# Stacked queries and keys in DRAM, fetched by one transfer per operand on SyncE's queue

## The chip, the cores and the metric

The kernel runs on one core of a Trainium2 chip. The metric is the device time of one execution in microseconds (us). The kernel before takes 1608.62 us, the median of 3 runs from 1608.35 to 1609.47 us.

## What is computed

Two encoder layers over 512 positions of 1024 channels in float32. Each layer normalizes its input, projects it once, and gives the parts to three branches: differential attention, a convolution module and Fourier mixing. The branches are projected, merged with sigmoid gates, projected again and added to the input; a SwiGLU feed-forward part follows. The change concerns the attention, which is, cut to what matters:

```python
q = u[..., o:o + WIDTH_A].reshape(b, s, N_HEADS_A, 2, D_COMP_A)   # 8 heads, 2 components of 32
k = ...                                                           # the same shape
q = apply_partial_rope(rmsnorm(q, qnorm_g[l]), cos, sin)
k = apply_partial_rope(rmsnorm(k, knorm_g[l]), cos, sin)
sc = jnp.einsum('bqhcd,bkhcd->bhcqk', qi, k) * scale
p = jax.nn.softmax(sc, axis=-1)
w = p[:, :, 0] - lam * p[:, :, 1]
att = jnp.einsum('bhqk,bkhe->bqhe', w, vf)
```

A head thus has two components of 32 channels, each with scores of its own.

## The kernel before

**Precision.** Matmuls run on float32 data that are rounded to a shorter format (`F32R`). Every operand is split into a high part, rounded by ScalarE (ACT), and a low part, the remainder, taken by VectorE (DVE); a product is the sum of high times high, high times low and low times high. For most products these are three matmuls that accumulate in one PSUM bank. For the scores it is one matmul: a component has only 32 channels, so three blocks of 32 are stacked on the 96 partitions of the operand. The queries are stacked as high, low, high and the keys as high, high, low, and one matmul of contraction 96 gives the three products' sum.

**How the stack is made.** `qk_post` normalizes and rotates queries (which = 0) and keys (which = 1), and four steps `turn(gp)`, one for each pair of heads, transpose 128 channels to a tile of 128 channels by 512 positions, split it into two `at` tiles (L163 on ACT, L164 on DVE), and store each to a DRAM tile `dqk` of its own (L849, 256 KB). `stack(h)` then fills, for each of a head's two components, a tile `qst` and a tile `kst`: each by three loads of 32 rows of 512 (L866, 64 KB), one for each block. In all there are 32 stores and 192 loads over the two layers, 12 loads for a head. All of them are issued by SyncE (SP), one instruction after the other.

**What shares SP's queue.** `chunk` loads the weights in chunks of 512 KB (`wr`, L204) from the same queue. A chunk is split too: ACT rounds it (L209). For even chunks DVE takes the remainder (L211). For odd chunks of the part with attention, ACT writes the negative of the rounded chunk (L331) and GpSimd (POOL) issues a transfer that adds the weights to it in place (`wl`, L332). POOL's transfers have a DMA queue of their own (q0 in the profile), those of SP another (q1).

**Buffers.** There are 3 buffers each of `qst` and `kst`, 5 of `at`, 3 of `wr`. A head needs two of `qst` and two of `kst`, so a load waits until TensorE (PE) has used up an older tile: the tiles of a head's first component can be fetched while the head before is still at work, those of its second component only when the head before lets a tile go, shortly before they are used. The `at` buffers go round: after the last stores they serve the exponentials of the scores (L951 on ACT), which must wait until the stores from the buffer have landed.

**What sets the order.** Each engine takes its instructions in the order in which the program's scheduler wrote them, and waits in that order. Attention is woven into the matmuls of the Fourier branch and of the gates: heads start at fixed places between those, `load(h)` is placed ahead of the first scores of head h, and on PE the score matmul `s<-kst,qst` (L127, called from `scores`) stands between matmuls `main<-X,wh` that have nothing to do with it. PE can't go past it. SP's instructions also wait for semaphores that eight lanes share (`DMAHW0` to `DMAHW7` below), each of which an earlier transfer of the same lane must have released.

Of the kernel before, what the change touches and what calls it, by code (L numbers as in the profile page):

```python
# [9 lines left out]
F32 = mybir.dt.float32  # L10
# [6 lines left out]
P = 128  # L17
L = 2
D = 1024
T = 512  # L20
# [15 lines left out]
QS = ("sync",) * 4  # L36
# [58 lines left out]
class Hybrid:  # L95
# [693 lines left out]
    def qk_post(self, l, which, banks):  # L789
        nc = self.nc  # L790
        qs = []
        names = ("rq", "rqs") if which == 0 else ("rk", "rks")
        tabs = []
        for i in range(2):
            tab = self.small(NT * 8, f"tab{i}")
            nc.vector.tensor_tensor(
                out=tab.rearrange("p (t d) -> p t d", d=8), in0=self.rope[:, i],
                in1=self.par(l, names[i]).unsqueeze(1).to_broadcast([P, NT, 8]), op=ALU.mult,
            )
            tabs.append(tab)  # L800
        for tt in range(NT):
            q = self.slot("A")
            nc.scalar.copy(q, banks[tt])
            sq = self.slot("M")
            nc.scalar.activation(sq, q, AF.Square)
            q3 = q.rearrange("p (m d) -> p m d", d=DC)
            sums = self.small(16, f"qs{tt}", 1)
            f = self.small(16, f"qf{tt}", 1)
            fa = self.small(16, f"qa{tt}", 1)
            nc.vector.tensor_reduce(  # L810
                out=sums, in_=sq.rearrange("p (m d) -> p m d", d=DC), axis=AX.X, op=ALU.add
            )
            nc.scalar.activation(f, sums, AF.Abs_reciprocal_sqrt, bias=self.eps, scale=1.0 / DC)
            nc.vector.tensor_scalar(
                out=sums, in0=sums, scalar1=1.0 / DC, scalar2=EPS, op0=ALU.mult, op1=ALU.add
            )
            nc.vector.scalar_tensor_tensor(out=fa, in0=f, scalar=-0.5, in1=f, op0=ALU.mult, op1=ALU.mult)
            nc.vector.tensor_tensor(out=fa, in0=fa, in1=sums, op=ALU.mult)
            nc.vector.scalar_tensor_tensor(out=f, in0=fa, scalar=1.5, in1=f, op0=ALU.add, op1=ALU.mult)
            nc.vector.tensor_tensor(  # L820
                out=q3, in0=q3, in1=f.unsqueeze(2).to_broadcast([P, 16, DC]), op=ALU.mult
            )
            ta3 = self.small(P, "ropea", RB).rearrange("p (m d) -> p m d", d=8)
            tb3 = self.small(P, "ropeb", RB).rearrange("p (m d) -> p m d", d=8)
            c8 = tabs[0][:, tt * 8 : (tt + 1) * 8].unsqueeze(1).to_broadcast([P, 16, 8])
            nc.vector.tensor_tensor(out=ta3, in0=q3[:, :, 0:8], in1=c8, op=ALU.mult)
            for o, i in ((0, 4), (4, 0)):
                s4 = tabs[1][:, tt * 8 + o : tt * 8 + o + 4].unsqueeze(1).to_broadcast([P, 16, 4])
                nc.vector.tensor_tensor(out=tb3[:, :, o : o + 4], in0=q3[:, :, i : i + 4], in1=s4, op=ALU.mult)
            nc.vector.tensor_tensor(out=q3[:, :, 0:8], in0=ta3, in1=tb3, op=ALU.add)  # L830
            qs.append(q)
        gc = self.small(1, f"gc{which}")
        self.after(nc.vector.tensor_scalar_mul(
            gc, self.par(l, "gkc" if which else "gqc"), 1.0 if which else DC ** -0.5
        ))
        out = []

        def turn(gp):
            ps = self.bank("att")
            for tt in range(NT):  # L840
                self.pin(
                    nc.tensor.transpose(  # L842
                        ps[:, tt * P : (tt + 1) * P], qs[tt][:, gp * P : (gp + 1) * P], self.ident
                    )
                )
            pair = []
            for i, src in enumerate(self.split_to(ps, "at", scale=gc)):
                d = self.dram.tile([P, T], F32, tag=f"qk{which}{gp}{i}", name=self.nm("dqk"))
                getattr(nc, QS[1]).dma_start(d, src.bitcast(F32))  # L849
                pair.append(d)  # L850
            out.append(pair)

        for gp in range(4):
            self.later(self.t + QKT + gp * 2000, "qk", lambda gp=gp: turn(gp))
        return out

    def stack(self, h):
        hp, h2 = divmod(h, 2)
        out = []
        for c in range(2):  # L860
            row = []
            for which, order in ((0, (0, 1, 0)), (1, (0, 0, 1))):
                dst = self.slot("kst" if which else "qst", F32R)
                lo = h2 * 64 + c * 32
                for r, hl in enumerate(order):
                    getattr(self.nc, QS[0]).dma_start(  # L866
                        dst[r * 32 : (r + 1) * 32, :].bitcast(F32), self.scr[which][hp][hl][lo : lo + 32, :]
                    )
                row.append(dst)
            out.append(row)  # L870
        return out
# [458 lines left out]
```

## Time and profile before

| | us |
|---|---|
| median of 3 runs | 1608.62 |
| the profiled execution | 1605.44 |
| its span, first to last instruction | 1603.7 |
| PE busy in the span | 1585.8 (99%) |
| DVE busy | 1307.9 (82%) |
| ACT busy | 869.9 (54%) |

The profiled execution's time lies 1.74 us above its span and 3.2 us below the median. In the profile an engine's name is followed by the line of the kernel, the operation, and the tiles (written<-read). PE is the matmul part of TensorE, PEld its weight load; SPq and POOLq are the parts of SP and POOL that issue transfers. A transfer has a start (its issue) and a landing. The granted clock of TensorE was 0.999 in the mean.

### The profile page before, as it was taken

Reading aid. Unit: us, or ns where it says so; the run is one execution under the profiler, and the core shown is the slowest. Engines: PE = TensorE matmul, PEld = TensorE weight load, DVE = VectorE, ACT = ScalarE, POOL = GpSimd, SP = SyncE. Lnnn points to the kernel's source line nnn. Section 1 sums busy time; section 2 is a strip of 40 time slices with the busy share of each in tenths; the row PEclk is TensorE's granted clock in tenths of the full one; section 3 lists DMA queues with packets and bytes.
Section 4 is the critical chain, followed back from the end, with each engine's and each line's share of the span. In section 5 each row is a group of like instructions: output and inputs, shape, how many; then the busy total and the mean of one; then the engine's idle time right before and its main releaser. Section 6 shows DMA issues by size and latency. Waiting matters only on the chain.

```text
span 1603.7 us, 24440 instructions
## 1 busy us (share of the span) xinstructions
PE 1585.8 (99%) x9104; PEld 1387.5 (87%) x9104; DVE 1307.9 (82%) x2388; ACT 869.9 (54%) x1419; POOL 183.5 (11%) x162
## 2 busy tenths in 40 slices
PE   9999999999999999999999999999999999999999
PEld 7888888787889898999888888887878898989998
DVE  6999999785897786858779999986758978778684
ACT  6546566873575453635443565568635754536351
POOL 1000010113330000000200000020233300000000
PEclk9999999999999999999999999999999999999999
DMA  6557365454554554547432664555455635546361
GB/s 223 170 164 202 79 164 150 117 132 112 165 149 115 146 134 140 139 109 191 123 118 81 192 186 113 135 146 125 107 120 155 167 94 156 133 133 158 90 159 66
DMA packets 80471, 222.85 MB, mean 139 GB/s; under 512 B 11216, under 2 KB 12368, under 8 KB 80352
## 3 DMA queue, kind: packets, MB, share of 16 engines
q1 hardware_dynamic: 67392, 175.59, 34.9%
q0 software_dynamic: 12528, 45.17, 16.2%
q8 instruction: 72, 1.18, 0.3%
q10 hardware_dynamic: 432, 0.53, 0.1%
q14 instruction: 47, 0.39, 0.1%
HBM read 207.35 MB, written 13.89 MB: 138 GB/s over the span
## 4 chain that ended last, share of the span: by engine, by line
PE 95%; DVE 2%; DMA 1%; ACT 1%; issue 0%; SPq 0%; ACTq 0%
PE main L127 57%; PE s L343 9%; PE main L343 9%; PE att L343 8%; PE s L127 4%; PE att L127 3%; PE oth L127 3%; PE att L137 2%; DMA wraw<-in_w 0%; PE att L842 0%; DVE A L161 0%; DMA kst<-dqk 0%; SPq L866 0%; DMA wr<-in_w 0%; PE oth L137 0%
## 5 line engine op out<-in xcount | busy, mean ns | idle before, releaser
L209 ACT CAST wh<-wr 128x1024 fp32r<-128x1024 f32 x178 | 186.1, 1049 | 244.4 <-PE main L127 127.3
L127 PE MATMUL main<-X,wh 128*128 128x512 f32 x864 | 278.4, 395 | 0.0
L211 DVE TENSOR_TENSOR wl<-wr,wh 128x1024 fp32r<-128x1024 f32 x138 | 176.6, 1280 | 36.7 <-ACT wh L209 36.1
L127 PEld LDWEIGHTS main<-X,wh 128*128 128x128 f32 x864 | 160.8, 188 | 32.3 <-issue 0.3
L1127 DVE SCALAR_TENSOR_TENSOR cv<-cv,hcw,cv 128x497 f32<-128x497 f32 (+14 forms) x240 | 180.2, 751 | 0.9
L127 PE MATMUL main<-X,wl 128*128 128x512 f32 x432 | 169.7, 393 | 0.0
L127 PE MATMUL main<-act,wh 128*128 128x512 f32 (+1 forms) x520 | 161.8, 391 | 0.0
L951 ACT ACTIVATE at<-s,mx 128x512 f32<-128x512 f32 x128 | 87.9, 688 | 58.1 <-DVE mx L949 49.1
L127 PEld LDWEIGHTS main<-act,wh 128*128 128x128 f32 x520 | 96.2, 188 | 21.7 <-DVE M L652 0.6
L127 PE MATMUL main<-A,wh 128*128 128x512 f32 x320 | 107.7, 393 | 0.0
L127 PE MATMUL main<-att,wh 128*128 128x512 f32 x320 | 100.0, 393 | 3.0 <-ACT att L160 3.0
L310 POOL DMA_DIRECT2D wlo<-in_w x44 | 37.7, 857 | 561.8 <-DVE V L653 166.2
L949 DVE TENSOR_REDUCE mx<-s 128x1 f32<-128x512 f32 x128 | 86.5, 682 | 18.5 <-PE s L127 17.9
L127 PE MATMUL main<-act,wl 128*128 128x512 f32 (+1 forms) x260 | 101.4, 391 | 0.0
L127 PE MATMUL main<-wh,X 128*128 128x512 f32 x288 | 96.7, 392 | 0.0
L127 PEld LDWEIGHTS main<-X,wl 128*128 128x128 f32 x432 | 81.4, 188 | 16.5
L332 POOL DMA_DIRECT2D wl<-in_w x40 | 34.5, 862 | 518.8 <-ACT wl L331 357.1
L127 PE MATMUL main<-cv,wh 128*128 128x512 f32 x240 | 76.8, 392 | 0.0
L127 PEld LDWEIGHTS main<-att,wh 128*128 128x128 f32 x320 | 59.7, 188 | 17.4 <-ACT att L160 3.5
L127 PE MATMUL main<-A,wl 128*128 128x512 f32 x192 | 74.4, 390 | 0.0
L127 PEld LDWEIGHTS main<-A,wh 128*128 128x128 f32 x320 | 59.7, 188 | 11.9
L127 PEld LDWEIGHTS main<-wh,X 128*128 128x128 f32 x288 | 53.9, 188 | 11.1
(371 smaller groups left out, 4190.4 us busy)
## 6 DMA issues: line engine op xcount, KB each, us to landing
wr<-in_w SPq DMA_DIRECT2D x222, 512.0 KB, 3.8
wlo<-in_w POOLq DMA_DIRECT2D x44, 512.0 KB, 5.6
wl<-in_w POOLq DMA_DIRECT2D x40, 512.0 KB, 7.7
cv<-in_w SPq DMA_DIRECT2D x80, 256.0 KB, 4.9
dqk<-at SPq DMA_DIRECT2D x32, 256.0 KB, 4.7
qst<-dqk SPq DMA_DIRECT2D x96, 64.0 KB, 2.3
kst<-dqk SPq DMA_DIRECT2D x96, 64.0 KB, 2.0
V<-in_xT SPq DMA_DIRECT2D x8, 256.0 KB, 6.9
```

Source lines behind the costliest of these rows:

```text
L127: return self.pin(self.nc.tensor.matmul(out, lhsT=lhsT, rhs=rhs, start=start, stop=stop))
L137: self.pin(self.nc.tensor.transpose(ps[:, s], src[:, s], self.ident))
L209: nc.scalar.copy(hi, raw)
L211: nc.vector.tensor_tensor(out=lo, in0=raw, in1=hi.bitcast(F32), op=ALU.subtract)
L310: nc.gpsimd.dma_start(l2, src2, accum_op=ALU.add)
L332: self.nc.gpsimd.dma_start(lo, src, accum_op=ALU.add)
L343: self.nc.tensor.matmul(ps, lhsT=a[:, s], rhs=b, start=start and k == ks[0] and i == 0, stop=last and i == 2, skip_group_check=True,)
L949: nc.vector.tensor_reduce(out=mx, in_=ps, axis=AX.X, op=ALU.max, negate=True)
L951: nc.scalar.activation(e, ps, AF.Exp, bias=mx, accum_out=z1 if c else z0)
L1127: ins = nc.vector.scalar_tensor_tensor(out=acc[:, a:b], in0=g[:, a + d : b + d], scalar=w[:, t : t + 1], in1=acc[:, a:b], op0=ALU.mult, op ...
```

## The change

`turn(gp)` stores into one DRAM tile of three blocks of 128 rows, in the order in which the stack wants them: high, low, high for queries, high, high, low for keys. The high part is therefore stored twice: three stores of 256 KB for each pair of heads and operand, 48 in all in place of 32. `stack(h)` then fetches each `qst` and each `kst` tile by one transfer of 192 KB: 64 loads in place of 192. Its source is a pattern of 3 blocks by 32 rows by 512 numbers, where the blocks lie 256 KB apart, and its destination 96 partitions by 512. Queue and engine stay the same, and so does everything else.

```diff
-            pair = []
-            for i, src in enumerate(self.split_to(ps, "at", scale=gc)):
-                d = self.dram.tile([P, T], F32, tag=f"qk{which}{gp}{i}", name=self.nm("dqk"))
-                getattr(nc, QS[1]).dma_start(d, src.bitcast(F32))
-                pair.append(d)
-            out.append(pair)
+            pair = self.split_to(ps, "at", scale=gc)
+            d = self.dram.tile([3, P, T], F32, tag=f"qk{which}{gp}", name=self.nm("dqk"))
+            for r, i in enumerate((0, 0, 1) if which else (0, 1, 0)):
+                getattr(nc, QS[1]).dma_start(d[r], pair[i].bitcast(F32))
+            out.append(d)
...
-            for which, order in ((0, (0, 1, 0)), (1, (0, 0, 1))):
+            for which in range(2):
                 dst = self.slot("kst" if which else "qst", F32R)
                 lo = h2 * 64 + c * 32
-                for r, hl in enumerate(order):
-                    getattr(self.nc, QS[0]).dma_start(
-                        dst[r * 32 : (r + 1) * 32, :].bitcast(F32), self.scr[which][hp][hl][lo : lo + 32, :]
-                    )
+                self.nc.sync.dma_start(
+                    dst[0:96, :].bitcast(F32), self.scr[which][hp][:, lo : lo + 32, :]
+                )
```

On PE, ACT, DVE and POOL the instructions stand in the same order as before; only the lines after the change move up by two. On SP the order changes at three kinds of places.

The first is SP's queue where the keys of the first head are fetched, in layer 1. `dqk_1161` holds the first pair's keys' high part and `dqk_1163` the low part, `dqk_1187` and `dqk_1189` those of the second pair, `dqk_1215` the third pair's. Before:

```order
L849 DMA dqk_1163<-at_1158 128x512 [waits DMAHW6_49,DVE_49]
L849 DMA dqk_1189<-at_1184 128x512 [waits DMAHW7_49,DVE_49]
L866 DMA kst_1373<-dqk_1161 32x512 [waits DMAHW4_49,DMAHW0_49]
L866 DMA kst_1373<-dqk_1161 32x512 [waits DMAHW1_49]
L866 DMA kst_1381<-dqk_1161 32x512 [waits DMAHW2_49]
L866 DMA kst_1381<-dqk_1161 32x512 [waits DMAHW3_49]
L866 DMA kst_1373<-dqk_1163 32x512 [waits DMAHW6_49]
L866 DMA kst_1381<-dqk_1163 32x512 [waits DMAHW5_49]
```

And now, where `dqk_1161` holds all three blocks of the first pair, `dqk_1187` of the second, and `dqk_1215` of the third:

```order
L849 DMA dqk_1161<-at_1157 128x512 [waits DMAHW2_49,Activation_49]
L849 DMA dqk_1161<-at_1157 128x512 [waits DMAHW3_49]
L849 DMA dqk_1187<-at_1183 128x512 [waits DMAHW4_49,Activation_49]
L849 DMA dqk_1187<-at_1183 128x512 [waits DMAHW5_49]
L849 DMA dqk_1161<-at_1158 128x512 [waits DMAHW6_49,DVE_49]
L849 DMA dqk_1187<-at_1184 128x512 [waits DMAHW7_49,DVE_49]
L204 DMA wr_2047<-in_w 128x1024 [waits DMAHW0_49,DVE_49]
L864 DMA kst_1371<-dqk_1161 96x1x512 [waits DMAHW3_49,DMAHW6_49,DMAHW2_49,DMAHW1_49]
L864 DMA kst_1375<-dqk_1161 96x1x512
L864 DMA kst_1613<-dqk_1161 96x1x512
L849 DMA dqk_1215<-at_1211 128x512 [waits DMAHW4_49,Activation_49]
L849 DMA dqk_1215<-at_1211 128x512 [waits DMAHW5_49]
```

The first load of keys now waits for the first pair's three stores, the last of which is fifth in the queue, and a chunk of weights, which stood behind the nine loads, stands ahead of them.

The second kind of place is every later head. Here is SP's queue in layer 2 where the tiles of the seventh head's second component are fetched (`qst_11514`, `kst_11518`) and behind them those of the eighth head's first (`qst_11761`). Before:

```order
L204 DMA wr_12287<-in_w 128x1024 [waits DMAHW7_49,DMAHW2_49,Activation_49]
L866 DMA qst_11514<-dqk_9315 32x512 [waits DMAHW3_49,PE_49]
L866 DMA qst_11514<-dqk_9317 32x512 [waits DMAHW4_49]
L866 DMA qst_11514<-dqk_9315 32x512 [waits DMAHW5_49]
L866 DMA kst_11518<-dqk_9597 32x512 [waits DMAHW6_49]
L866 DMA kst_11518<-dqk_9597 32x512
L866 DMA kst_11518<-dqk_9599 32x512 [waits DMAHW0_49]
L866 DMA qst_11761<-dqk_9315 32x512 [waits DMAHW1_49,PE_49]
L866 DMA qst_11761<-dqk_9317 32x512 [waits DMAHW2_49]
```

Now, with the seventh head's second component in `qst_11398` and `kst_11400` and the eighth's first in `qst_11641` and `kst_11643`:

```order
L204 DMA wr_12159<-in_w 128x1024 [waits DMAHW3_49,Activation_49]
L864 DMA qst_11398<-dqk_9251 96x1x512 [waits DMAHW7_49,PE_49]
L864 DMA kst_11400<-dqk_9533 96x1x512 [waits DMAHW0_49]
L864 DMA qst_11641<-dqk_9251 96x1x512 [waits DMAHW1_49,PE_49]
L864 DMA kst_11643<-dqk_9533 96x1x512 [waits DMAHW2_49]
L204 DMA wr_12202<-in_w 128x1024 [waits DMAHW4_49,DVE_49]
```

The chunk of weights stands where it stood, and four loads take the place of twelve; each pair still begins with a wait for PE.

The third place is on ACT, whose order is the same but whose waits are not: the exponentials of the first scores in layer 1, which write `at` buffers that stores to DRAM have read. Before:

```order
L951 ACTIVATE at_1456,z_453_1450<-s_1452,mx_1454 128x512 [waits DMAHW7_49,DMAHW0_49,DVE_49]
L951 ACTIVATE at_1462,z_454_1451<-s_1458,mx_1460 128x512 [waits DMAHW2_49,DVE_49,Activation_49]
L951 ACTIVATE at_1517,z_453_1450<-s_1513,mx_1515 128x512 [waits DMAHW3_49,DVE_49]
L951 ACTIVATE at_1523,z_471_1512<-s_1519,mx_1521 128x512 [waits DMAHW4_49,DVE_49]
L951 ACTIVATE at_1598,z_453_1450<-s_1594,mx_1596 128x512 [waits DMAHW5_49,DVE_49]
```

Now:

```order
L949 ACTIVATE at_1448,z_445_1442<-s_1444,mx_1446 128x512 [waits DMAHW7_49,DMAHW6_49,DVE_49]
L949 ACTIVATE at_1454,z_446_1443<-s_1450,mx_1452 128x512 [waits DMAHW4_49,DMAHW5_49,DVE_49,Activation_49]
L949 ACTIVATE at_1509,z_445_1442<-s_1505,mx_1507 128x512 [waits DMAHW3_49,DMAHW7_49,DMAHW2_49,DVE_49]
L949 ACTIVATE at_1515,z_463_1504<-s_1511,mx_1513 128x512 [waits DMAHW6_49,DMAHW0_49,DVE_49]
L949 ACTIVATE at_1590,z_445_1442<-s_1586,mx_1588 128x512 [waits DMAHW1_49,DVE_49]
```

The second exponential waited for one store of the third pair's high part (lane 2) and now waits for both of them (lanes 4 and 5); in SP's queue these stand right behind the three loads of keys, where three of them replace nine.

## The prediction

> **What bounds the kernel now.** I read the page first, then PE's waits, then DMA, then the timeline where the scores take their operands.
>
> ```profile
> span 1603.7 us, 24440 instructions
> PE 1585.8 (99%) x9104; PEld 1387.5 (87%) x9104; DVE 1307.9 (82%) x2388; ACT 869.9 (54%) x1419; POOL 183.5 (11%) x162
> ...
> PE s L127 <- DMA kst<-dqk: 3.0, 1, 3.0
> ```
>
> PE is busy 1585.8 of 1603.7 us, so only 17.9 us could be won by any means, and of these the only wait for the tiles that the change touches is one of 3.0 us. The 192 small loads are otherwise hidden. A change to them can win 3.0 us at most; it can lose more, since PE takes its instructions in order, and a score matmul whose tile comes late holds up everything behind it. A measurement can tell about 0.2%, 3.2 us, from no change. So the question is how late the tiles can come before PE notices, and when they come now.
>
> **The new load's price.** What the small loads and the engines of the DMA do:
>
> ```profile
> DMA to landing us min/median/max: 1.7/1.9/2.0
> ...
> DMA packets 441, 0.81 MB, mean 403 GB/s; under 512 B 48, under 2 KB 48, under 8 KB 441
> q1 hardware_dynamic: 441, 0.81, 104.5%
> ...
> DMA packets 80471, 222.85 MB, mean 139 GB/s; under 512 B 11216, under 2 KB 12368, under 8 KB 80352
> q0 software_dynamic: 12528, 45.17, 16.2%
> wr<-in_w SPq DMA_DIRECT2D x222, 512.0 KB, 3.8
> alt2f<-in_alt POOLq DMA_DIRECT2D x1, 1.0 KB, 5.9
> ```
>
> The first row is of five query loads in the quiet stretch from 160 to 164 us. The next two are of the stretch from 128.5 to 130.5 us, where stores fill all 16 engines: 441 − 48 = 393 packets of 2 KB in 2.0 us x 16 x 1.045, so a packet takes 85 ns. A small load of 64 KB is 32 such packets; on 16 engines it is two for each, 0.17 us, and the rest of its 1.9 us, 1.7 us, is fixed.
>
> How many engines will the new load use? The 692 transfers listed in the view of DMA issues (first and last quoted, 30 rows) leave 16 small closing packets each, 11,072; with 128 pieces of 32 B from one small load of parameters and 16 of 64 B from the last row, that makes the page's 11,216. So every transfer here runs on 16 engines, but every one also has a pattern that leads with 32 or 128 rows. The new source leads with 3 blocks that don't join up. Two readings fit the rows: transfers are always cut in 16 (**wide**), or they are cut along the leading count, which has been a multiple of 16 so far and is now 3 (**narrow**). I take narrow, at about 4 to 1: the source's 96 rows have no single stride, so the pattern would have to be rewritten to be cut in 16, and no row shows a pattern cut within its second count. Then a load is 32 packets on each of three engines, 32 x 0.085 = 2.7 us: queries land 1.7 + 2.7 = 4.4 us after their issue, and keys, issued at once behind on the same three engines, 7.1 us after it. Wide would be 96 / 16 x 0.085 = 0.5 us, keys after about 3 us; that and narrow are the price's two ends.
>
> The Trainium skill, "DMA: Bandwidth & Descriptors", section "Why a DMA increments its semaphore by 16 and not by 1", states that a transfer runs on the largest number of engines up to 16 that divides the leading counts of both its patterns. By that rule 3 and 96 leave 3 engines, the narrow sum below; the rows, all with multiples of 16, agree with it but test nothing else.
>
> What also runs on those engines: a `wl` transfer of POOL is 8 packets of 4 KB for each engine, and q0's 12,528 packets take 16.2% of 16 x 1603.7 us, 332 ns each, so 2.7 us come between. A `wr` issued just ahead is 32 KB for each engine, 16 x 85 ns = 1.4 us.
>
> **The heads.** A second component's load is issued when PE lets a tile go; its scores follow at a fixed place. The five shortest of these 14 leads, with POOL's transfers beside them:
>
> ```profile
> 217.13 1.25 SPq L866 DMA_DIRECT2D qst<-dqk  x3
> 217.50 0.85 POOL L332 DMA_DIRECT2D wl<-in_w  x1 [12.61 <-ACT wl L331]
> 226.58 0.40 PE L127 MATMUL s<-kst,qst 96*128 96x512 f32 x1
> ...
> 245.06 0.85 POOL L332 DMA_DIRECT2D wl<-in_w  x1 [10.36 <-ACT wl L331]
> 246.04 1.38 SPq L866 DMA_DIRECT2D qst<-dqk  x3
> 256.24 0.48 PE L127 MATMUL s<-kst,qst 96*128 96x512 f32 x1
> ...
> 1010.96 1.25 SPq L866 DMA_DIRECT2D qst<-dqk  x3
> 1011.51 0.86 POOL L332 DMA_DIRECT2D wl<-in_w  x1 [10.77 <-DVE rt L955]
> 1020.19 0.40 PE L127 MATMUL s<-kst,qst 96*128 96x512 f32 x1
> ...
> 1103.35 0.33 SPq L204 DMA_DIRECT2D wr<-in_w  x1
> 1103.69 0.87 POOL L332 DMA_DIRECT2D wl<-in_w  x1 [20.71 <-ACT wl L331]
> 1103.77 3.53 SPq L866 DMA_DIRECT2D qst<-dqk  x3
> 1112.64 0.47 PE L127 MATMUL s<-kst,qst 96*128 96x512 f32 x1 [3.01 <-DMA kst<-dqk]
> ...
> 1129.86 1.56 SPq L866 DMA_DIRECT2D qst<-dqk  x3
> 1131.77 0.86 POOL L332 DMA_DIRECT2D wl<-in_w  x1 [3.45 <-ACT wl L331]
> 1138.57 0.39 PE L127 MATMUL s<-kst,qst 96*128 96x512 f32 x1
> ```
>
> The leads are 9.45, 10.20, 9.23, 8.87 and 8.71 us. A narrow pair beside a `wl` lands 7.1 + 2.7 = 9.8 us after its issue. It is late by 0.4, 0 (0.3 with the rest of a chunk ahead of it), 0.6, then with the chunk at 1103.35 ahead 9.8 + 1.4 − 8.87 = 2.3 on top of today's 3.0, and 1.1: 4.7 us in all. The other nine leads are longer; the shortest is this, with no `wl` beside it:
>
> ```profile
> 954.72 1.25 SPq L866 DMA_DIRECT2D qst<-dqk  x3
> ...
> 965.14 0.40 PE L127 MATMUL s<-kst,qst 96*128 96x512 f32 x1
> ```
>
> I cost these nine at nothing, their cover being the lead, 10.4 us and more against 9.8. First components have over 20 us and are free. The weights behind the loads come later as well; they are covered by the buffers of `wr`, `wh` and `wl`, and PE waits for no `wr` now.
>
> **The first head of each layer.**
>
> ```profile
> 129.39 5.34 SPq L866 DMA_DIRECT2D kst<-dqk  x9
> 138.20 0.63 PE L127 MATMUL s<-kst,qst 96*128 96x512 f32 x2
> 140.28 0.69 ACT L951 ACTIVATE at<-s,mx 128x512 f32<-128x512 f32 x1
> 150.55 0.60 PE L137 MATMUL att<-ident,at 128*128 128x128 f32 x4
> ...
> 924.60 0.78 SPq L866 DMA_DIRECT2D kst<-dqk  x2
> 932.69 0.63 PE L127 MATMUL s<-kst,qst 96*128 96x512 f32 x2
> 934.77 0.69 ACT L951 ACTIVATE at<-s,mx 128x512 f32<-128x512 f32 x1
> 946.50 0.63 PE L137 MATMUL att<-ident,at 128*128 128x128 f32 x4
> ```
>
> A store of 256 KB is 8 packets for each engine, 0.68 us; 16 more of them cost the DMA 11 us, spread over stretches where PE doesn't read them. But the first key load, which started when the first store had landed, now waits for the fifth in layer 1 and the fourth in layer 2: 2.7 and 2.0 us later, at 132.1 and 926.6. Both components' keys are needed at once, in two loads on the same three engines: 1.7 + 5.4 = 7.1 us, 139.2 and 933.7, against second scores at 138.4 and 932.9. PE waits 0.8 in each; with the chunk of weights that now stands ahead in layer 1, 1.0. Together 1.8 us.
>
> The second exponential is a wait that the change adds. It needs two stores that stand behind three loads of keys, on three engines 8.1 us, behind a `wl` and themselves 1.4 us: 132.1 + 1.7 + 8.1 + 2.7 + 1.4 = 146.0, where it started at 140.28; in layer 2, with a chunk between, 926.6 + 15.3 = 941.9 against 934.77. ACT is 5.7 and 7.1 us late, and behind it wait casts of weights, copies out of PSUM and the Fourier branch's splits, for which DVE waits. PE needs the exponential itself only 10.3 and 11.7 us after it (the transposes at 150.55 and 946.50), so the price lies between nothing, as ACT is idle 46% of the time, and all of it, 12.8 us. I take 1.5 in each, 3.0, nearer to nothing, since the leads are longer than the delays.
>
> **The sum.** 4.7 + 1.8 + 3.0 = 9.5 us on the profiled 1605.44: 1614.9. The runs' median lies 3.2 above that execution, so 1618.1; I say 1618. SP itself issues 112 instructions less, worth nothing where it waits for PE.
>
> **The rivals.**
>
> Wide, chance 0.18: 16 engines. Then a pair lands with one fixed time and 1 us of packets, and SP issues two for six. The wait of 3.0 shrinks by what issues cost, about 1 us, as a `wl` still stands ahead: 1608.62 − 1 = 1607.6; the doubled store costs the first heads nothing, 132.1 + 1.7 + 1 = 134.8 being well before 138.2. Even all 3.0 us would give 1605.6, under 0.2%. So it is no change, not slower. For it: every transfer so far has 16 engines. The skill's same page, "Rules for kernel authors", advises to join small transfers, saying that under 64 KB one pays mostly overhead; by that rule the wide end is the sum, and the trace shows the overhead (1.7 of 1.9 us) but off PE's path.
>
> Narrow but hidden, 0.14: queries and keys slip between POOL's packets, 7.1 us hold instead of 9.8, and ACT's lag is absorbed. Then only 1103.77 costs, 0 to 2.3 us, and the first heads up to 1.8: 1608.6 to 1612.7. For it: leads of 8.7 and more exceed 7.1. Against: today's pair there took 8.9 with a `wl` beside it.
>
> Weights late, 0.04: two pairs hold three engines for 10.9 us, and a `wr` behind them lands after 14.7 in place of 3.8. If buffers covered only 11 us of it, 3.7 us at each of 14 groups is 52 us, 1670. It decides once casts wait for `wr`; none does now in attention.
>
> The forecast, narrow and seen by PE, keeps 0.64.
>
> **How the numbers follow.** The forecast's ends are 1611 (only 1103.77 costs) and 1628 (ACT's lag comes through in full, 9.8 more). The range adds no change at its low end: 1608 to 1628. Faster 0.03, from wide; same 0.22 (0.15 of wide and half of the hidden case); slower 0.75.
>
> **What would show it.** Narrow: small closing packets fall by 13 for each of 64 loads; `qst` and `kst` land 4 us or more after issue in quiet; PE's waits name `kst<-dqk` at several heads, the most at the second exponential's layer starts and near 1109. Wide: landings near 2.3 us and the 3.0 gone or smaller. If landings are long and PE doesn't wait, my leads are wrong; if ACT's exponentials wait for `dqk` and PE doesn't, the 3.0 was nothing. The forecast is wrong if the span grows with PE's busy time and not with its idle time.

## The result, and the profile after

| | before | after |
|---|---|---|
| median of five runs each, us | 1608.35 | 1647.59 |
| lowest and highest | 1605.65, 1609.47 | 1642.96, 1653.65 |
| the profiled execution | 1605.44 | 1642.96 |
| its span | 1603.7 | 1640.9 |
| PE busy, PE idle in the span | 1585.8, 17.9 | 1595.6, 45.3 |
| mean granted clock of TensorE | 0.999 | 0.993 |

The change makes the kernel slower by 2.5% (ratio 1.0249, 95% interval 1.0231 to 1.0266). The forecast had the sign and the mechanism, and was far off in size: 9.5 us were priced, and the profiled span grew by 37.2, of which 27.4 are idle time of PE and 9.8 busy time.

The page of the kernel after, its head and its line of DMA packets:

```profile
span 1640.9 us, 24278 instructions
PE 1595.6 (97%) x9104; PEld 1392.1 (85%) x9104; DVE 1309.8 (80%) x2388; ACT 869.9 (53%) x1419; POOL 183.4 (11%) x162
...
DMA packets 79893, 227.01 MB, mean 138 GB/s; under 512 B 8592, under 2 KB 9744, under 8 KB 79776
```

There are now 692 − 128 + 16 = 580 transfers. On 16 engines each would leave 580 x 16 + 144 = 9,424 packets under 512 B; 13 fewer for each of 64 loads is 8,592, the number in the row. The loads run on three engines. Next, PE's waits (in us in total, times and longest):

```profile
PE s L127 <- DMA kst<-dqk: 25.1, 9, 6.3
PE s L127 <- issue: 3.3, 1, 3.3
...
PE s L127 <- ACT at L949: 1.2, 2, 0.8
PE s L127 <- ACT ar L974: 1.0, 1, 1.0
```

The one wait of 3.0 us for a key tile has become nine of 25.1 us together. Two more are waits for key tiles too, though the profile names something else. The 3.3 us put down to "issue" belong to the second score matmul of the first head, shown further below. The 1.0 us put down to `ar` are at this matmul:

```profile
1111.85 0.47 PE L127 MATMUL s<-kst,qst 96*128 96x512 f32 x1 [0.98 <-ACT ar L974]
```

PE's sequencer waits there for the semaphore of the key tile (sixth head of layer 2, second component), whose last update comes at 1111.76, while the copy to `ar` ended at 1111.53. For exponentials PE waits no longer than before.

PE has 9,104 matmuls in both traces, in the same order, so each matmul of the kernel after can be compared with the same one before. The first score matmul of a component starts at these times:

| | before | after | later by |
|---|---|---|---|
| layer 1, head 1, second component | 138.43 | 146.88 | 8.45 |
| layer 1, head 2 | 165.15 | 175.34 | 10.19 |
| layer 1, head 8, second component | 343.04 | 358.06 | 15.02 |
| layer 2, head 2 | 959.83 | 984.75 | 24.92 |
| layer 2, head 8, second component | 1138.57 | 1175.70 | 37.13 |

So layer 1 loses 10.2 us at its first head and 4.8 at the other seven; layer 2's first head 9.9 (about 1 of it arises between the two layers) and its others 12.2. From there to the end nothing is added. The first head of layer 1, from the timeline of the kernel after:

```profile
137.47 2.19 SPq L864 DMA_DIRECT2D kst<-dqk  x3
...
139.76 6.07 SPq L849 DMA_DIRECT2D dqk<-at  x6
...
140.31 0.87 POOL L332 DMA_DIRECT2D wl<-in_w  x1 [16.92 <-ACT wl L331]
...
143.07 0.50 PE L127 MATMUL s<-kst,qst 96*128 96x512 f32 x1 [3.66 <-DMA kst<-dqk]
...
146.88 0.76 PE L127 MATMUL s<-kst,qst 96*128 96x512 f32 x1 [3.31 <-issue]
...
147.44 1.05 PE L127 MATMUL main<-X,wh 128*128 128x512 f32 x2
```

The key loads are issued at 137.47 where 132.1 was forecast, a `wl` stands beside them, and the second tile is there 9.4 us after the loads' issue instead of 7.1. The last row shows something else: two `main` matmuls take 1.05 us, where they took 0.62 before the stall. That is TensorE's clock. The windows view of this stretch and the next, and behind them one of the kernel before, after its wait of 3.01 us (PEclk is the granted clock, x a count of instructions):

```profile
core 0: us, PE busy (x) PEld busy (x) DVE busy (x) ACT busy (x) POOL busy (x), PEclk, DMA share, GB/s
143.60:150.40 6.80, 3.52 (x8) 2.81 (x9) 3.41 (x5) 0.78 (x2) 0.00 (x0) 0.50 0.97 258
150.40:157.20 6.80, 6.80 (x38) 5.88 (x37) 3.62 (x12) 3.68 (x6) 0.00 (x0) 1.00 0.41 139
```

```profile
1113.50:1116.90 3.40, 3.40 (x17) 3.30 (x16) 1.21 (x3) 2.12 (x5) 0.61 (x1) 0.50 0.86 228
```

The kernel before has one stretch of 3.4 us at half the clock; the kernel after has four, of 6.8, 6.8, 3.4 and 6.8 us, each beginning in a stall or right behind it (143.6, 952.5, 1048.1 and 1143.7 us). The prediction has no term for it. The Trainium skill, "TensorE: Matmul & The Clock Gate", sections "What's actually happening" and "Why this matters for your kernels", has the rule: the clock is halved and given back by windows of about 3.4 us that run on their own, and idle gaps of more than about 3 us should be avoided. The trace agrees on the 3.4 us.

A later head, the seventh of layer 2, where the kernel before had its one wait. The timeline of the kernel after:

```profile
1134.08 0.33 SPq L204 DMA_DIRECT2D wr<-in_w  x1
...
1134.42 0.87 POOL L332 DMA_DIRECT2D wl<-in_w  x1 [21.92 <-ACT wl L331]
...
1134.50 0.72 SPq L864 DMA_DIRECT2D qst<-dqk  x1
...
1135.27 0.69 SPq L864 DMA_DIRECT2D kst<-dqk  x1
...
1146.68 0.77 PE L127 MATMUL s<-kst,qst 96*128 96x512 f32 x1 [6.31 <-DMA kst<-dqk]
```

The pair is usable 12.2 us after its issue, where the prediction has 9.8 + 1.4 = 11.2 for this place.

### The profile page after: what moved, and what is told of

Same layout as the page of the kernel before. It is cut to its first block, busy times and chain, and to the rows that moved or that the text cites. A ratio compares the mean times of both kernels' runs of the same rounds, so it can differ in the third digit from the quotient of the medians.

```text
span 1640.9 us, 24278 instructions
## 1 busy us (share of the span) xinstructions
PE 1595.6 (97%) x9104; PEld 1392.1 (85%) x9104; DVE 1309.8 (80%) x2388; ACT 869.9 (53%) x1419; POOL 183.4 (11%) x162
## 2 busy tenths in 40 slices
DMA packets 79893, 227.01 MB, mean 138 GB/s; under 512 B 8592, under 2 KB 9744, under 8 KB 79776
## 4 chain that ended last, share of the span: by engine, by line
PE 83%; DMA 9%; issue 3%; DVE 3%; ACT 2%; SPq 0%; POOL 0%; POOLq 0%; DVEq 0%; ACTq 0%
PE main L127 47%; PE s L343 9%; PE main L343 9%; PE att L343 8%; DMA kst<-dqk 5%; PE att L127 3%; PE s L127 3%; PE oth L127 3%; DMA dqk<-at 1%; PE att L137 1%; DMA wr<-in_w 1%; DMA wl<-in_w 1%; DMA V<-in_xT 0%; DVE A L161 0%; SPq L864 0%
## 5 line engine op out<-in xcount | busy, mean ns | idle before, releaser
L127 PE MATMUL s<-kst,qst 96*128 96x512 f32 x128 | 54.7, 430 | 30.8 <-DMA kst<-dqk 25.1
```

Of the source, the lines that this page charges most:

```text
L127: return self.pin(self.nc.tensor.matmul(out, lhsT=lhsT, rhs=rhs, start=start, stop=stop))
```

## The experiments

Theory A: the loads' three engines make the tiles late, at the first heads and, beside POOL's adding transfers, at later heads, and TensorE's clock adds to each long stall. Its rivals were that the doubled stores do it (B), or that one transfer of 192 KB is slow on any engines (C).

**Rows ahead.** The changed kernel with the source's dimensions in another order:

```diff
-    dst[0:96, :].bitcast(F32), self.scr[which][hp][:, lo : lo + 32, :]
+    dst[0:96, :].bitcast(F32), self.scr[which][hp][:, lo : lo + 32, :].rearrange("r p t -> p r t")
```

> The changed kernel with one thing altered: the load's source runs over the 32 rows first and over the 3 blocks second, so that its pattern leads with 32 and not with 3. The same bytes come by the same 64 transfers at the same places of SP's queue, the doubled stores stay, and the contraction's 96 rows are permuted alike in queries and keys, which leaves the result as it is. Theory A (the loads run on three DMA engines and so land late; PE waits for them and its clock is halved after the longer waits): the loads run on 16 engines, small closing packets rise from 8,592 to 580 x 16 + 144 = 9,424, PE's waits for kst<-dqk shrink from 25.1 us to about 3, the granted clock is 0.5 nowhere or once, and the time comes back to that of the kernel before within 3 us, 1605 to 1611. Theory B (the doubled stores and the waits for the buffers that they read are the cause): the time stays at 1640 or above. Theory C (one transfer of 192 KB lands late whatever its engines, for instance because a tile is usable only when all of it has come): about half of the loss stays, 1620 or above.

Measured: 1606.76, ratio to before 0.9994 (0.9985 to 1.0002). The page's packets and PE's wait:

```profile
DMA packets 80726, 227.01 MB, mean 141 GB/s; under 512 B 9425, under 2 KB 10577, under 8 KB 80609
```

```profile
PE s L127 <- DMA kst<-dqk: 2.1, 1, 2.1
```

All of the loss is gone with the order of one pattern. B and C fall: the doubled stores and the transfers of 192 KB are all still there.

**Stores doubled, loads as before.**

```diff
-    self.nc.sync.dma_start(
-        dst[0:96, :].bitcast(F32), self.scr[which][hp][:, lo : lo + 32, :]
-    )
+    for r in range(3):
+        self.nc.sync.dma_start(
+            dst[r * 32 : (r + 1) * 32, :].bitcast(F32), self.scr[which][hp][r, lo : lo + 32, :]
+        )
```

> The changed kernel's stacked DRAM tiles with all 48 stores, but each tile fetched as before by three loads of 32 rows, 192 in all. Theory A: the stores alone cost only what they hold up at the first head of each layer, 0 to 3 us: 1608 to 1611, with PE's idle time about 18 us as before. Theory B: the stores carry the loss, 1640 or above. Theory C: as A.

Measured: 1607.16, ratio 0.9996 (0.9988 to 1.0005). The extra stores by themselves cost nothing that can be measured.

**Two loads a tile, stores as before.** A load of 64 rows (for keys the high part twice) and one of 32; all lead with 32:

```diff
+    two = d[0, lo : lo + 32, :].unsqueeze(1).to_broadcast([32, 2, T]) if which else (
+        d[:, lo : lo + 32, :].rearrange("r p t -> p r t")
+    )
+    self.nc.sync.dma_start(dst[0:64, :].bitcast(F32), two)
+    self.nc.sync.dma_start(dst[64:96, :].bitcast(F32), d[which, lo : lo + 32, :])
```

> The 32 stores of the kernel before, so no doubled high part, and two loads for each tile, of 64 and 32 rows, 128 in all, whose patterns all lead with 32 rows (the keys' high part is read twice by a source that repeats a row). Theory A: 1605 to 1609, and the difference to the kernel with 64 loads that lead with 32 rows is the price of the doubled stores, under 3 us; small closing packets are (500 + 128) x 16 + 144 = 10,192. Theory B: also 1605 to 1609, as the stores are those of before. Theory C: between, as two thirds of a tile come by one transfer: 1612 to 1625.

Measured: 1608.51, ratio 1.0000 (0.9991 to 1.0009), 10,192 packets under 512 B as forecast. With 192, 128 or 64 loads the time is the same, as long as each runs on 16 engines.

**The first heads alone mended, and the converse.**

```diff
+    src = self.scr[which][hp][:, lo : lo + 32, :]
+    if h == 0:
+        src = src.rearrange("r p t -> p r t")
+    self.nc.sync.dma_start(dst[0:96, :].bitcast(F32), src)
```

> The changed kernel, with the source that leads with 32 rows in the first head of each layer only (8 of the 64 loads, 3 of them with stores around them in each layer); the other 14 heads keep the source that leads with 3 blocks. Theory A: in the changed kernel PE lost about 13 us of idle time at the two first heads and some 7 us by the halved clock after these stalls; both go and the later heads' stay, so the time falls by 15 to 20 us, to 1627 to 1633, and half clock remains only behind the later stalls of about 3 us and more (two stretches in the changed kernel). Theory B: no change, 1647. Theory C: a smaller fall, under 8 us.

Measured: 1640.63 (four runs, 1633.46 to 1643.70), only 7 us less: a miss for A's number. The converse has `if h > 0`:

> The converse of the kernel in which only the first heads' loads lead with 32 rows: here the first head of each layer keeps the source that leads with 3 blocks (8 loads), and the other 56 loads lead with 32 rows. Compared matmul by matmul with the kernel before, the changed kernel falls behind by 10.4 us at the first head of layer 1 and by 8.9 us at that of layer 2, and by some 17 us at later heads. Theory A (each load on three engines delays by itself): the first heads keep their loss, 15 to 20 us, the later heads lose nothing: 1623 to 1628. The run with only the first heads mended came out just 7 us below the changed kernel; if that was the first heads' true share (rival D: the loss is not local, later heads make up or lose what the first ones leave), this kernel lies 7 us above the kernel before, about 1615.

Measured: 1627.09, ratio 1.0129 (1.0115 to 1.0143): the first heads alone cost 19.8 us, as A said, and D falls. Why the other kernel gained less is seen in its waits:

```profile
PE s L127 <- DMA kst<-dqk: 18.2, 6, 7.0
PE s L127 <- ACT at L950: 5.0, 4, 2.3
```

Where first heads' loads are quick, PE waits 1.5 and 2.3 us there for exponentials (147.67 and 954.04 us); the third key load in the queue is still on three engines, and the stores whose buffers the exponentials need stand behind it. In the changed kernel this wait lay under the longer one for the keys. And the stalls that remain are longer (6.97 us where the changed kernel has 6.31) and meet more windows of the clock: half clock lasts 30.6 us in this run against 23.8 in the changed kernel. A stall of 2.48 us cost 3.4 us at half clock here, one of 2.26 us at the same head none in the changed kernel. The 7 us are thus not the first heads' share.

**Keys asked for earlier.** The changed kernel with a fourth key buffer and keys ahead of queries, so that only one of the two slow loads waits for PE:

```diff
-        "X": 16, "A": 8, "B": 8, "V": 8, "att": 8, "cv": 8, "at": 5, "ar": 2, "M": 4, "rb": 1, "qst": 3, "kst": 3,
+        "X": 16, "A": 8, "B": 8, "V": 8, "att": 8, "cv": 8, "at": 5, "ar": 2, "M": 4, "rb": 1, "qst": 3, "kst": 4,
...
-            for which in range(2):
+            for which in (1, 0):
...
-                row.append(dst)
+                row.insert(0, dst)
```

> The changed kernel, sources that lead with 3 blocks, but with four kst buffers and keys asked for ahead of queries. Theory A: after PE lets a tile go only one slow load stands on the path, not two behind each other on the same three engines; that is about 4 us less of some 12, so the later heads' stalls (about 17 us of loss) go but for 0 to 3 us, and the first heads keep their 15 to 20 us: 1622 to 1632. Rival F: the three engines are short of throughput as a whole, so that an earlier issue gains nothing: 1640 or above.

Measured: 1633.92 (1631.15 to 1637.85), just over A's 1632. The parts came out otherwise than the sum: compared matmul by matmul with before, the heads 2 to 8 lose 0.8 us in layer 1 and 1.1 in layer 2 (17.0 in the changed kernel), and the first heads 13.1 and 13.8 (10.4 and 8.9 there). So lead decides at the later heads, and F falls. The first heads got worse by 3 and 5 us, with 10.2 and 13.7 us of half clock there against 6.8 and 6.8 in the changed kernel; why is open.

**POOL's adding transfers taken away.** Both the changed kernel and the one with rows ahead, with

```diff
         self.heads(l, self.t + ATT0, ATT)
-        self.by_dma = True
+        self.by_dma = False
```

> The changed kernel without POOL's adding transfers in the part with attention: the low half of every weight chunk is taken by DVE there, as it is for even chunks (the result stays the same). To be read against the kernel that has the same edit and loads that lead with 32 rows; the instructions of these two stand in the same order. Theory A with POOL's part (the later heads' 17 us arise because a wl transfer shares the three engines and takes a pair's landing from about 8 us to 12, above leads of 9 to 12 us): the later heads lose 0 to 4 us, the first heads, which have no wl beside them, 15 to 21 as before: 17 to 25 us above the partner. Rival I (a pair on three engines takes about 12 us in this part whether wl is there or not): 33 to 40 us above the partner, as in the changed kernel.

> The partner: all loads lead with 32 rows, and no adding transfers of POOL in the part with attention. DVE, busy 82% of the span before, takes some 29 more subtractions of 128 x 1024, about 1 us each. All theories: no stall names the loads; the time is that of the kernel before plus what DVE's added work costs, 1605 to 1625.

Measured: 1633.94 for blocks ahead, 1623.39 for rows ahead. The edit by itself costs 16.6 us with rows ahead (1606.76 before it); three engines cost 10.6 us where they cost 40.8 with POOL's transfers (1647.59 against 1606.76). That is less than either theory said. Matmul by matmul, the scores of heads 2 to 8 lose nothing against the partner, in either layer; the first heads lose 2.6 and 3.8, not 15 to 21. The other 4 us lie where both kernels wait for the same length but the clock's windows fall otherwise (13.7 us of half clock against 6.8 near 335 us, 3.4 against none near 1290). The edit also moves scores: with blocks ahead the leads of second components are 9.8 to 13.7 us here, where the shortest before was 8.7, so the fall from 40.8 to 10.6 isn't shown to be POOL's part alone. The landings themselves, in the next section, don't depend on the leads. Layer 1's first head without POOL's transfers, loads on three engines:

```profile
132.02 2.19 SPq L864 DMA_DIRECT2D kst<-dqk  x3
```

```profile
138.51 0.40 PE L127 MATMUL s<-kst,qst 96*128 96x512 f32 x1
141.33 0.47 PE L127 MATMUL s<-kst,qst 96*128 96x512 f32 x1 [2.42 <-issue]
```

The keys are issued at 132.02, which is the 132.1 of the prediction, and PE waits 2.4 us, for the second key tile, which lands at 141.24. My expectation that no `wl` lies beside the first heads was wrong: in the changed kernel one is issued at 122.53 and one at 140.31. Without them the five stores issued ahead of the keys land by 133.2 us; with them the six ahead of the keys land by 138.0, and the keys are issued later.

**Idle matmuls in the stalls.** The changed kernel with matmuls that are thrown away, ahead of the score matmuls that wait:

```diff
+            for _ in range(fill[c]):
+                self.mm(ps, *self.fill, True, True)
             self.mm(ps, qs[0:96, qt * P : (qt + 1) * P], ks[0:96, :], True, True)
```

> The changed kernel with idle matmuls added on PE: 101 matmuls that multiply operands at hand into the bank which the next score matmul overwrites, put ahead of the score matmuls that had to wait 1.8 us and more (14 and 13 in the first head of layer 1, 16 and 6 in that of layer 2, 8, 10, 24 and 10 in four later heads). They leave the output as it is and take about 0.23 us each, 23 us in all, inside 27 us of waiting. Theory G (half of the loss beside the stalls is TensorE's clock, which was granted at half speed for 3.4 or 6.8 us after a stall of about 2.7 us and more; PE that stays busy keeps it): half clock disappears or is down to one stretch, and the time falls by 5 to 10 us although PE has 23 us more to do: 1637 to 1643. Rival H (the halved clock follows from something else in these stretches, such as traffic or stores): the stretches at half clock stay and the time is the same or longer, 1647 to 1655. The scheduler places a few other instructions differently for the added work, so single microseconds say nothing here; the profile's clock decides.

Measured: 1653.99, slower, against G's number. Its time decides nothing about G: the scheduler had moved other score matmuls ahead, and these stalled (5.0, 4.9 and 3.8 us). The cleaner form, on the kernel where only first heads are slow:

> A cleaner test of the clock. The kernel with idle matmuls came out slower, 1654: at the heads that were filled the stalls and most of the half clock were gone, but the scheduler, which counts the added matmuls, had put other score matmuls nearer to their loads, and these stalled by 3.8 to 5.0 us, with half clock behind each. Here the base is the kernel in which only the first head of each layer has the source that leads with 3 blocks (1627.1 us, 10.2 and 6.8 us of half clock behind the first heads' stalls of 3.9, 4.3, 3.5 and 2.2 us), so that no other head can stall; ahead of those four score matmuls stand 15, 16, 13 and 7 idle matmuls, 11.6 us of work at 0.23 us each inside 13.9 us of waiting, which leave the output as it is. Theory G (the stall takes the clock): half clock at the first heads is gone or down to one stretch of 3.4 us, and the time falls by 4 to 8 us, to 1619 to 1623, although PE has 11.6 us more to do. Rival H (traffic or stores take it): it stays, and the time with it: 1627 to 1632.

Measured: 1624.18 (1622.95 to 1624.75), 2.9 us less than without the 51 matmuls; G said 4 to 8 less. At the first head of layer 1, the kernel without and the kernel with them:

```profile
141.60:151.80 10.20, 4.71 (x10) 3.46 (x11) 3.96 (x8) 1.56 (x4) 0.00 (x0) 0.50 0.90 256
```

```profile
142.00:148.80 6.80, 6.15 (x27) 4.77 (x26) 6.68 (x11) 2.25 (x5) 0.00 (x0) 1.00 0.99 292
```

All 17.0 us of half clock at the first heads are gone, with the DMA as busy as it was. What is missing to G's number is at least in part a moved score matmul again, which stalls at 326.86:

```profile
PE s L130 <- DMA kst<-dqk: 5.8, 4, 4.3
```

and has 6.8 us of half clock behind it. Rival H, that traffic takes the clock, falls by the kernel with 101 matmuls as well: behind its stall of 4.94 us the clock is half while the DMA is all but idle (its share is 0.04).

```profile
364.40:367.80 3.40, 3.09 (x7) 2.51 (x8) 1.10 (x4) 0.93 (x3) 0.00 (x0) 0.50 0.04 18
```

**A better kernel.** Rows ahead, a fourth key buffer, keys ahead of queries (the two diffs above together):

> All loads lead with 32 rows, and there are four kst buffers in place of three, with a tile's keys asked for ahead of its queries: the keys of a second component then no longer wait for PE to let a tile go, only the queries do. With all loads leading with 32 rows but three buffers, PE still waited 2.1 us for a tile at 1114 us and had half the clock for 3.4 us there. Theory A: the lead is what decides; with one load instead of two in the 8.9 us this wait goes, with its clock: 2 to 4 us under the kernel with three buffers, 1603 to 1605, half clock only elsewhere if at all. Rival E: the wait there is set by the transfers of POOL and the weights beside it, not by what SP has to fetch: no change, 1606 to 1608.

Measured: 1604.81, ratio 0.9988 (0.9979 to 0.9997). The clock isn't halved anywhere between start and end, and at the place of the one wait PE waits 1.65 us in place of 3.01:

```profile
1111.59 0.47 PE L127 MATMUL s<-kst,qst 96*128 96x512 f32 x1 [1.65 <-ACT at L949]
```

The profile puts this down to an exponential, but the scores take turns in two PSUM banks, and the exponential that frees this one ended at 1107.02. PE's sequencer waits there for the semaphore of the query tile, and that gets its last update at 1111.50. So PE still waits for a tile, now the queries, which are issued here:

```profile
1104.75 0.55 SPq L864 DMA_DIRECT2D qst<-dqk  x1
```

Does the buffer do this alone? The kernel before, with 192 small loads, the fourth buffer and keys first:

> The kernel before with its 192 small loads and 32 stores, but four kst buffers in place of three and a tile's keys asked for ahead of its queries. This tells whether the gain of the kernel with one load per tile, 32 rows ahead, and four kst buffers (1604.8) comes from the buffer alone. Theory A: yes, the wait of 3.0 us at 1112.6 us and the 1.7 us of halved clock behind it go here as well: 1603 to 1605.5. Rival: three loads at 1.3 us of issue for each tile still come too late: 1606 to 1608.

Measured: 1608.27, ratio 1.0003 (0.9994 to 1.0012): no. Its wait at that place is still there, now for the queries:

```profile
PE s L127 <- DMA qst<-dqk: 3.1, 1, 3.1
```

```profile
1106.39 3.69 SPq L866 DMA_DIRECT2D qst<-dqk  x3
```

SP is at its three small loads of queries for 3.69 us there, and at the one load for 0.55. So one load per tile is worth about 3 us with the fourth buffer (1604.81 against 1608.27, or 0.9988 against 1.0003 of the kernel before), provided that it runs on 16 engines; without that buffer it is worth nothing that can be measured (0.9994 with rows ahead). Over the kernel before the gain is 0.12%, with an interval that ends just below 1.

## Why the prediction was right in kind and wrong in size

| term | priced, us | measured, us |
|---|---|---|
| second components at later heads | 4.7 | 17.0 (13.5 idle for key tiles, the rest about half clock) |
| first heads, both layers | 1.8 | 20.1 (13.0 idle for key tiles, 1.5 for the transposes ahead of them, the rest mostly clock) |
| exponentials behind the stores | 3.0 | 0 here; 1.5 and 2.3 where the keys are quick |
| TensorE's clock | not named | within the first two rows, 6.1 of PE's 9.8 us of busy time |

*Narrow* was right, and the leading count is the cause: 8,592 packets, and the whole loss undone by putting the rows ahead. The rule of the Trainium skill, "DMA: Bandwidth & Descriptors", section "Why a DMA increments its semaphore by 16 and not by 1", which gives 3 engines for a leading count of 3, agrees with every kernel: 8,592 with 64 narrow loads, 8,696 with 56, 9,320 with 8, 9,425 with none. The places were right too: PE waits for keys at the five heads that the prediction listed and at both first heads, and only for 0.4 and 1.0 us at two others, the sixth of each layer, which the prediction had put at nothing; the longest stall is at the pair with the chunk at 1103.35 ahead of it.

The first step that failed is the landing, "a narrow pair beside a `wl` lands 7.1 + 2.7 = 9.8 us after its issue". The path was right and both terms were too small. Here is a pair of the changed kernel, in layer 2, with neither a `wl` nor a chunk beside it (the timeline, then the DMA view from 1002.7 to 1010.4 us):

```profile
1002.71 0.72 SPq L864 DMA_DIRECT2D qst<-dqk  x1
1003.48 0.69 SPq L864 DMA_DIRECT2D kst<-dqk  x1
...
DMA packets 204, 0.42 MB, mean 55 GB/s; under 512 B 6, under 2 KB 6, under 8 KB 203
q1 hardware_dynamic: 203, 0.40, 16.3%
```

Two loads leave six small closing packets, three each. 203 packets in 16.3% of 16 x 7.7 us are 99 ns each, where the price has 85. The landing is read from the semaphores in the trace: a load on 16 engines makes 16 updates there and one on three engines four, the last when the tile is complete. This pair's keys land 8.1 us after its issue, and by the estimate 1.7 + 64 x 0.099 = 8.0. So 1.0 us of what is missing is the pair's own. Beside a `wl` that is issued from 1.1 us before the pair to 2.1 us after it, the keys of eight second components land after 11.4 to 13.9 us, so the `wl`, with the chunks around it, adds 3.3 to 5.8 us where 2.7 was priced. In the kernel without POOL's transfers the keys of all 14 second components land after 8.3 to 9.7 us, chunks or not, and none comes late. The shortest leads were 8.7 to 10.2 us, so the longer landings turned 4.7 us into 13.5 of idle time.

The second is the first heads. The prediction moved the key loads from 129.4 to 132.1 by counting the stores ahead of them, and put no `wl` beside them. They were issued at 137.47; without `wl` at 132.02, and then the two heads cost 2.6 and 3.8 us, clock included, nearer to the 1.0 and 0.8 that were priced. What was missing ahead of the issue is a chain with POOL's traffic in it: the query loads are slow too, and stores behind them land late. The store issued at 125.82 took 9.0 us, where one issued at 125.08 before took 4.2. The landing was priced too short here as well: layer 1's second key tile lands 9.3 us after the first load's issue, and 9.2 without `wl`, where the price is 7.1.

The third is a term that is missing. The trace of the kernel before had it in view, 17 matmuls in 3.4 us at half clock behind its only long stall. Over the kernels here PE's busy time goes with the time at half clock between start and end: 1584.6 us with none, 1585.8 with 3.4, 1588.5 with 6.8, 1593.6 and 1595.6 with 23.8, 1599.4 with 30.6. That is about 0.35 to 0.6 us for each us, and not all of it is clock, as matmuls next to a stall are longer too: those that ran at half clock in the changed kernel, set against the same ones before, make up 6.1 of its 9.8 us. With the clock, the one wait of 3.0 us of the kernel before was also worth more than the "3.0 us at most" of the first part, namely up to 3.0 + 3.4 / 2 = 4.7. The prediction would have counted as wrong a span that grows with PE's busy time; a quarter of the growth is that.

The lag of the exponentials was priced at 3.0 and came to nothing, because PE was waiting for keys in the same stretch; two delays beside each other were added. The reading behind the 3.0 was also wrong. The scores have two PSUM banks, so PE needs the second exponential first for the same component's next score, 4.7 us after its start in the kernel before (140.28 to 145.01), and not only for the transposes 10.3 us after it. That is where PE waits 1.5 and 2.3 us when the keys are quick. Of the rivals, wide and hidden are out, and weights late too, as none of PE's waits in attention names a chunk. The profiled execution lay 4.6 us below the median of its kernel's runs, against 3.2 for the kernel before; the changed kernel's runs scatter more (1642.96 to 1653.65), and their mean granted clocks fall with it from 0.993 to 0.987, probably because a stall that is a little longer or shorter gains or loses a whole window of the clock.

## What to carry to other kernels

Joining small loads can pay only if the joined pattern still leads with a count that spreads over all engines: put the 32 rows ahead of the 3 blocks, and count the small closing packets to see how many engines a transfer had. A transfer on few engines is priced with everything that shares those engines, adding transfers of GpSimd above all, and against the lead of each single use, not against the mean. And a stall of PE of over about 2 us is to be priced with the clock behind it, up to 1.7 us for each 3.4 us window.

## What the runs showed of the hardware that was not expected

The stall that takes the clock can be short, and its length alone doesn't decide: 2.01 us (blocks ahead, without POOL's transfers), 2.08 (rows ahead), 2.29 and 2.48 us were each followed by 3.4 us of half clock, 2.26 and 2.66 us in the changed kernel by none. With rows ahead, three gaps of 0.5, 0.7 and 0.7 us between 460.6 and 466.4 us were followed by 3.4 us too; in the kernel before, the same gaps were not. The rule of about 3 us, from the Trainium skill's "TensorE: Matmul & The Clock Gate" above, is not the least that these runs show. PE with matmuls to throw away in its stalls kept the clock, and the kernel got 2.9 us shorter with 11.6 us more work.

While only loads on three engines are moving, the DMA's line of shares stands at 1 and 2 tenths, 3 of 16 being 0.19. From the changed kernel's DMA view of 170.5 to 182 us, in 40 slices:

```profile
DMA  0000000122010121212955488976995799999764
```

A pair was issued at 170.98 and 171.75 and another behind it; packets begin some 1.5 us later, and from the middle on a chunk and a `wl` follow.
